# Gate and feature tiles of a decoder layer: wide products by the high weights, narrow ones by the low weights

## The chip, the core and the metric

The kernel runs on one core of a Trainium2 chip. The metric is the device time of one execution in microseconds (us); the time of a kernel is the median of its runs. The engines are TensorE (PE, with its weight loads PEld), VectorE (DVE), ScalarE (ACT), GpSimd (POOL) and SyncE (SP, which issues most of the DMAs). [...]

## What is computed

One layer of a decoder: one projection of the 256 tokens feeds three token mixers (A sparse attention over top-k keys, B dilated windows, C block-sparse, which at 256 tokens is plain causal attention), and a gate per channel merges them. Then come an output projection, a layer norm, a feed-forward part and a second norm.

```
proj = x @ w_in[i]                                    # 256 x 1024 by 1024 x 3528
aq, ak, av, iq, ik, iw, bq, bk, bv, cq, ck, cv = jnp.split(proj, SPLIT_POINTS, axis=-1)
o_a, o_b, o_c = dsa_mixer(...), dilated_mixer(...), moba_mixer(...)
gates = jax.nn.sigmoid(x @ w_gate[i]).reshape(bsz, s_len, N_BRANCH, D_MODEL)
merged = (gates[:, :, 0] * (o_a @ w_br_a[i]) + gates[:, :, 1] * (o_b @ w_br_b[i])
          + gates[:, :, 2] * (o_c @ w_br_c[i]))
x = layer_norm(ALPHA * x + merged @ w_out[i], ln1_g[i], ln1_b[i])
h = jnp.square(jax.nn.relu(x @ w_up[i])) @ w_down[i]
ple = jax.nn.sigmoid(x @ w_ple_gate[i]) * (p[i] @ w_ple[i])
x = layer_norm(ALPHA * x + h + ple, ln2_g[i], ln2_b[i])
```

## The kernel before

All products are float32, made of three products of a shorter type (F32R): every operand is split into a high part and a low part, and high x high, high x low and low x high are summed (function prod, L133 to L135). The low x low product is left out.

The weights come in units of 128 x 1024 (a unit is 128 output channels for all eight k-tiles of 128 inputs). Class Weights moves a unit through: SP loads it (tile raw, L71), ScalarE rounds it to the high part (whi, L75), VectorE and POOL subtract to the low part (wlo, L79; VectorE takes 640 of 1024 columns, POOL the rest). It runs four units ahead of its use; raw and part (whi and wlo) have five buffers each.

x stands transposed in SBUF, tokens along the columns: xh and xl, [128, 8, 256] each. A tile of 128 gate channels (24 of them, fill with "g") or of 128 feature channels (queries and keys, feat) is gemm: for each of the eight k, three products of 256 columns into one half of a PSUM bank of pool mm, which has three banks. ScalarE takes a gate tile out of PSUM through a tanh (L238). A feature tile is split from PSUM into a high half by ScalarE and a low half by VectorE (q_pair L214 and L215, k_pair L225 and L226).

In the up projection (L681 to L686) the tiles are built in another way: x1 holds high and low halves side by side, the high weights multiply both at once in a product of 512 columns, the low weights multiply the high half in one of 256, and VectorE adds the two halves of the bank.

Around the tiles lies attention. logits makes the logits of two heads (L271) into banks b0 to b2. VectorE adds the bias table T and takes the maxima (L357 for mixer B, in slots, L341 for C and A, in head); ScalarE takes the exponentials (L366, L344) and scales them (L333); in mixer B POOL adds up three groups in between (L368 and L369). TensorE transposes the result (L310 to L312), multiplies by the values (L317 to L320), and VectorE adds the halves (L323). Tables T are loaded by SP from DRAM (L182). VectorE also finds the 64 largest entries of the index of mixer A (topk, eight rounds of MAX and MATCH_REPLACE, then am, L440 to L444); POOL adds am to T for the heads of A (ta, L497 and L498).

The order of the instructions on each engine is not the program's: a scheduler of the framework lays out all engines by a model of their times and its priorities, and fixes one order per engine, in which the engines then run, waiting for one another by semaphores. TASKS sets the order of the weight units.

Of the kernel before, what the change touches and what calls it, by code (L numbers as in the profile page):

```python
# [11 lines left out]
F32 = mybir.dt.float32  # L12
F32R = mybir.dt.float32r
ALU = mybir.AluOpType
AF = mybir.ActivationFunctionType
AX = mybir.AxisListType
# [4 lines left out]
S = 256  # L21
KT = D // 128
# [71 lines left out]
def hybrid_layer(ctx: ExitStack, tc: tile.TileContext, x0, xn, pT, wqk, wva, wvb, wg, wbc, wba,  # L94
                 wout, wup, wdq, wdn, wpg, wple, lnrow, rel, onehot, pick, out):
    nc = tc.nc
    pe, act, dve, pool = nc.tensor, nc.scalar, nc.vector, nc.gpsimd
# [8 lines left out]
    W = Weights(tc, raw, part)  # L106
# [24 lines left out]
    def prod(ps, a, b, first, last):  # L131

        pe.matmul(ps, lhsT=a[0], rhs=b[0], start=first, stop=False)  # L133
        pe.matmul(ps, lhsT=a[0], rhs=b[1], start=False, stop=False)  # L134
        pe.matmul(ps, lhsT=a[1], rhs=b[0], start=False, stop=last)  # L135

    def gemm(ps, units, xs, k=0):

        for u in units:
            hi, lo = W.get(u)  # L140
            for o in range(0, hi.shape[1], 128):
                prod(ps, (hi[:, o:o + 128], lo[:, o:o + 128]), xs[k], k == 0, k == len(xs) - 1)
                k += 1
# [5 lines left out]
    right = lambda n, b: one.enter_context(tc.tile_pool(name=n, bufs=b, side="right"))  # L149
    p1, k1, kp = (right(n, b) for n, b in (("p1", 1), ("k1", 2), ("kp", 3)))  # L150

    xh = p1.tile([128, KT, S], F32R, name="xh")
    xl = p1.tile([128, KT, S], F32R, name="xl")
    xs = [(xh[:, k], xl[:, k]) for k in range(KT)]
    n_u = [0]

# [5 lines left out]
    G = pm.tile([128, 24, S], F32, name="G")  # L162
    pm.tile([128, 8], F32, name="apart")
    u_q = [[] for _ in range(FIRST)]

    u_g, u_bc, u_ba, u_out = [], [], [], []
# [38 lines left out]
    def mmbank(shape):  # L205
        t = mm.tile([128, 512], F32, name="mm", tag="mm")
        return t[:, 0:256] if shape == 256 else t
# [11 lines left out]
    def k_pair(a, b=None):  # L219


        k = (kp if b is None else k1).tile([128, 2, S], F32R, name="k", tag="k")
        for d, ps in ((slice(0, 128), a),) if b is None else ((slice(0, 64), a),
                                                             (slice(64, 128), b)):
            act.copy(k[d, 0], ps)  # L225
            dve.tensor_tensor(k[d, 1], ps, k[d, 0].bitcast(F32), op=ALU.subtract)  # L226
        return k

    n_g, n_c = [0], [0]

    def fill(what):


        for w in what:
            if w == "g":
                ps = mmbank(256)
                gemm(ps, u_g[n_g[0]], xs)
                act.activation(G[:, n_g[0]], ps, AF.Tanh, scale=0.5)  # L238
                n_g[0] += 1
                continue  # L240
            f = n_c[0]
            n_c[0] += 1
            hi, lo = W.get(u_bc[f][0])
            ps = mmbank(512).rearrange("p (i s) -> p i s", i=2)
            for i, (k0, k1) in enumerate(((3, 5), (5, 8))):
                for k in range(k0, k1):
                    c = slice((k - 3) * 128, (k - 2) * 128)
                    prod(ps[:, i], (hi[:, c], lo[:, c]), (op[:, k, 0], op[:, k, 1]), k == k0,
                         k == k1 - 1)
            g = G[:, 3 * f + 1:3 * f + 3]  # L250
            dve.scalar_tensor_tensor(g, g, 1.0, ps, op0=ALU.add, op1=ALU.mult)  # L251
            dve.tensor_tensor(g[:, 0], g[:, 0], g[:, 1], op=ALU.add)

    def feat(f):
        ps = mmbank(256)
        gemm(ps, u_q[f], xs)
        if f > 4:
            next(side, None)
        return ps

    def logits(q, k):


        ss = [next(ps_s)[:, 0:384] for _ in range(2)]
        with tc.high_priority(offset=500):
            for b in range(2):
                c = slice(b * 128, (b + 1) * 128)
                for i, (x, y) in enumerate(((1, 0), (0, 0), (0, 1))):
                    for h in (1, 0):
                        d = slice(64 * h, 64 * h + 64)  # L270
                        m = pe.matmul(ss[h][:, QC[b]], lhsT=q[d, x, c],  # L271
                                      rhs=k[d, y, 0:128 * (b + 1)], start=i == 0, stop=i == 2)
                        if b or i or not h:
                            tc.keep_in_program_order(m)
        return ss
# [3 lines left out]
    op = pm.tile([128, 8, 2, S], F32R, name="op")  # L279
# [108 lines left out]
    with ExitStack() as begin:  # L388
# [4 lines left out]
        with tc.high_priority(offset=1000):  # L393
# [4 lines left out]
            for k in range(KT):  # L398
                act.copy(xh[:, k], g0[:, k, 0:S])
                for a, b in cut[k]:  # L400
                    a = max(a, S)
# [4 lines left out]
        for k in range(KT):  # L406
            for i, (w, x) in enumerate(((sh, xh), (sh, xl), (sl, xh))):
                for f in range(FIRST):
                    pe.matmul(first[f], lhsT=w[:, k, 128 * f:128 * f + 128], rhs=x[:, k],  # L409
                              start=k == i == 0, stop=k == KT - 1 and i == 2)  # L410
        iq = [q_pair(ps, 0.125) for ps in first]
    tp, wk, wk2, sm = (right(n, b) for n, b in (("tp", 3), ("wk", 3), ("wk2", 2), ("sm", 6)))
    tab = bias_table()
    ps = feat(4)
    kI, kA = k_pair(ps[0:64], ps[0:64]), k_pair(ps[64:128], ps[64:128])

# [8 lines left out]
    for j in range(4):  # L425
        s = logits(iq[j], kI)
# [9 lines left out]
    def topk():  # L436
        for r in range(TOPK // 8):
            for b in range(2):
                m8 = sm.tile([128, 8], F32, name="m8", tag="m8")
                dve.max(m8, idx[:, QC[b]])  # L440
                dve.match_replace(idx[:, QC[b]], in_to_replace=m8, in_values=idx[:, QC[b]],
                                  imm_value=GONE)
            yield
        dve.tensor_scalar(am, idx, -2e38, -NEG, op0=ALU.is_gt, op1=ALU.mult)  # L444

    side = topk()
# [4 lines left out]
    for j in range(2):  # L451
        ps = feat(5 + 4 * j)
        k = k_pair(ps)
        fill("g")
        qs = []
        for g in range(3):
            qs.append(q_pair(feat(6 + 4 * j + g)))
            if g:
                fill("g")
        o = opair()  # L460
        Ts = [toeplitz(6 + 2 * j + h, 4) for h in range(2)]
        slots(qs, k, Ts, 1 + 2 * j, o)
        pair_out(o, 3 + j)
        fill("g")
# [6 lines left out]
    for j in range(3):  # L471
        ps = feat(13 + 2 * j)
        k = k_pair(ps)
        q = q_pair(feat(14 + 2 * j))
        s = logits(q, k)
# [12 lines left out]
    for j in range(3):  # L488
        q = q_pair(feat(19 + j))
        s = logits(q, kA)  # L490
# [152 lines left out]
    for b in range(2):  # L643
        t = slice(b * 128, (b + 1) * 128)
        for c in range(2):
            cs = slice(c * 512, (c + 1) * 512)
            ps = mmbank(512)
# [28 lines left out]
    for f in range(32):  # L676
        ps = mmbank(512).rearrange("p (b a t) -> p b a t", b=2, a=2)
        hi, lo = W.get(u_up[f][0])
        cs = [slice(k * 128, (k + 1) * 128) for k in range(KT)]
        for k in range(KT):  # L680
            pe.matmul(ps, lhsT=hi[:, cs[k]], rhs=x1[:, :, k], start=k == 0, stop=False)  # L681
        for k in range(KT):
            pe.matmul(ps[:, :, 0], lhsT=lo[:, cs[k]], rhs=x1[:, :, k, 0], start=False,  # L683
                      stop=k == KT - 1)
# [11 lines left out]
        g = four[:, u % 2]  # L696
        act.activation(g[:, :, m], r, AF.Square)
        if m % 2 == 0:
            continue
        hi, lo, y = ((hQ[:, u, 0, 0], hQ[:, u, 0, 1], g[:, 0, 0:2]) if m == 1 else  # L700
                     (hQ[:, u, 1:3, 0], hQ[:, u, 1:3, 1], g[:, :, 2:4]))
# [87 lines left out]
    for i in range(early):  # L789
        x = order[i]  # L790
        hi, lo = W.get(u_dn[i])
# [7 lines left out]
    p1, p5, p6, p7 = (acc["P" + n] for n in "1567")  # L799
# [25 lines left out]
    for b in range(2):  # L825
        for c in range(len(CUT[b])):
            cs = slice(*CUT[b][c])
# [110 lines left out]
```

## Time and profile before

| | |
|---|---|
| time of the runs, median (lowest to highest of 3) | 446.04 us (444.22 to 446.31) |
| time of the profiled execution | 445.0 us |
| its span, from the first to the last instruction | 443.2 us |
| mean granted TensorE clock | 0.994 |
| busy: TensorE, its weight loads | 97%, 88% of the span |
| busy: VectorE, ScalarE, POOL | 75%, 61%, 23% of the span |
| moved by DMA | 84.28 MB, 190 GB/s |

A line of the profile names the source line, the engine, the operation, the output and input tiles (buffer numbers left out), the shape and the count; then come the busy time in us, the mean of one in ns, and the idle time ahead of it with what ended it. The timeline and the chain of waits give start and length in us. TensorE's matmuls are pipelined: one starts while the last is still draining, so their lengths overlap.

### The profile page before, as it was taken

The numbers are of one execution on the slowest core, as the hardware profiler recorded it, in microseconds if no ns is written. First come the engines' busy times: TensorE is split into PE (matmuls) and PEld (weight loads), VectorE is DVE, ScalarE is ACT, GpSimd is POOL, SyncE is SP. The second block draws the span as 40 slices with busy tenths as digits, with TensorE's granted clock in tenths as the row PEclk, the third lists the DMA queues.
The fourth block names the chain that finished last, engine by engine and source line by source line (L and its number), as shares of the span: only waits on it lengthen the run. The fifth ranks groups of instructions, "written<-read, shape, count | busy, mean of one in ns | idle before, by whom it ended". The sixth has DMA issues, their size and how long they took to land.

```text
span 443.2 us, 7744 instructions
## 1 busy us (share of the span) xinstructions
PE 429.7 (97%) x2839; PEld 389.3 (88%) x2839; DVE 333.7 (75%) x601; ACT 270.7 (61%) x488; POOL 102.8 (23%) x99
## 2 busy tenths in 40 slices
PE   8999999998999999999999999999999999999992
PEld 8989999998999989999886888888888888888882
DVE  5867977536546568759958769999888978689956
ACT  6765366476877758756604657878877765455500
POOL 2764247378533545500001000000000000000001
PEclk9999999999999999999999999999999999999997
DMA  8895956448635326468870766567655364656502
GB/s 302 298 314 156 286 160 199 150 113 281 224 94 170 126 77 184 131 202 315 260 283 0 248 226 193 190 191 270 204 189 184 100 207 132 228 195 212 215 0 95
DMA packets 27146, 84.28 MB, mean 190 GB/s; under 512 B 2864, under 2 KB 6872, under 8 KB 26724
## 3 DMA queue, kind: packets, MB, share of 16 engines
q1 hardware_dynamic: 25872, 79.54, 54.4%
q10 hardware_dynamic: 1140, 4.19, 2.6%
q8 instruction: 22, 0.36, 0.3%
q14 instruction: 16, 0.13, 0.1%
q0 software_dynamic: 96, 0.06, 0.0%
HBM read 81.88 MB, written 1.90 MB: 189 GB/s over the span
## 4 chain that ended last, share of the span: by engine, by line
PE 89%; DVE 3%; issue 2%; DMA 2%; POOL 2%; ACT 1%; SPq 0%; POOLq 0%; DVEq 0%
PE mm L681 13%; PE mm L133 12%; PE mm L135 12%; PE mm L134 12%; PE b L133 8%; PE b L135 8%; PE b L134 8%; PE mm L683 7%; PE b L271 3%; PE b L409 3%; DMA T<-tabd 1%; DMA pr<-in_pT_dram 1%; PE b L129 1%; DVE st L605 1%; DVE Y L622 1%
## 5 line engine op out<-in xcount | busy, mean ns | idle before, releaser
L75 ACT CAST whi<-raw 128x1024 fp32r<-128x1024 f32 (+3 forms) x147 | 148.0, 1013 | 81.2 <-issue 19.9
L79 DVE TENSOR_TENSOR wlo<-raw,whi 128x1024 fp32r<-128x1024 f32 (+5 forms) x147 | 156.1, 1076 | 42.7 <-ACT whi L75 38.7
L79 POOL TENSOR_TENSOR wlo<-raw,whi 128x384 fp32r<-128x384 f32 (+3 forms) x58 | 78.5, 1359 | 83.2 <-ACT whi L75 74.0
L133 PE MATMUL mm<-xh,whi 128*128 128x256 f32 x336 | 95.0, 283 | 1.0 <-DVE G L251 1.0
L135 PE MATMUL mm<-xh,wlo 128*128 128x256 f32 x336 | 95.6, 285 | 0.0
L134 PE MATMUL mm<-xl,whi 128*128 128x256 f32 x336 | 94.7, 282 | 0.0
L133 PEld LDWEIGHTS mm<-xh,whi 128*128 128x128 f32 x336 | 63.3, 189 | 1.5 <-DVE G L251 1.2
L681 PE MATMUL mm<-x,whi 128*128 128x512 f32 x256 | 64.1, 392 | 0.0
L135 PEld LDWEIGHTS mm<-xh,wlo 128*128 128x128 f32 x336 | 63.3, 188 | 0.8
L134 PEld LDWEIGHTS mm<-xl,whi 128*128 128x128 f32 x336 | 63.3, 188 | 0.3
L612 POOL TENSOR_TENSOR rs<-rs,half 128x1 f32<-128x1 f32 x4 | 4.1, 1028 | 244.5 <-DVE rs L611 244.5
L681 PEld LDWEIGHTS mm<-x,whi 128*128 128x128 f32 x256 | 46.1, 189 | 8.3
L683 PEld LDWEIGHTS mm<-x,wlo 128*128 128x128 f32 x256 | 34.9, 190 | 2.5
L683 PE MATMUL mm<-x,wlo 128*128 128x256 f32 x256 | 35.7, 282 | 0.0
L134 PE MATMUL b<-wlo,hT 128*128 128x512 f32 (+1 forms) x88 | 33.4, 380 | 0.0
L135 PE MATMUL b<-whi,hT 128*128 128x512 f32 (+1 forms) x88 | 33.4, 379 | 0.0
L133 PE MATMUL b<-whi,hT 128*128 128x512 f32 (+1 forms) x88 | 31.9, 379 | 0.0
L686 DVE TENSOR_REDUCE r<-mm 128x256 f32<-128x512 f32 x32 | 22.0, 687 | 6.0 <-PE mm L683 6.0
L742 DVE TENSOR_TENSOR raw<-raw 128x1024 f32<-128x1024 f32 x12 | 14.7, 1222 | 9.0 <-DMA raw<-in_wdq_dram 9.0
L133 PEld LDWEIGHTS b<-whi,hT 128*128 128x128 f32 x88 | 16.6, 188 | 3.1
L135 PEld LDWEIGHTS b<-whi,hT 128*128 128x128 f32 x88 | 16.5, 188 | 3.2
L134 PEld LDWEIGHTS b<-wlo,hT 128*128 128x128 f32 x88 | 16.5, 188 | 3.1
(194 smaller groups left out, 782.0 us busy)
## 6 DMA issues: line engine op xcount, KB each, us to landing
raw<-in_wup_dram SPq DMA_DIRECT2D x32, 512.0 KB
raw<-in_wg_dram SPq DMA_DIRECT2D x24, 512.0 KB
raw<-in_wdn_dram SPq DMA_DIRECT2D x20, 512.0 KB
raw<-in_wqk_dram SPq DMA_DIRECT2D x18, 512.0 KB
raw<-in_wdq_dram SPq DMA_DIRECT2D x12, 512.0 KB
raw<-in_wout_dram SPq DMA_DIRECT2D x8, 512.0 KB
raw<-in_wpg_dram SPq DMA_DIRECT2D x8, 512.0 KB
T<-tabd SPq DMA_DIRECT2D x24, 128.0 KB
```

The lines of the kernel that those rows point to most:

```text
L75: nc.scalar.copy(hi, r)
L79: e.tensor_tensor(lo[:, c], r[:, c], hi[:, c].bitcast(F32), op=ALU.subtract)
L129: pe.transpose(t[:, 0:128], ident, ident)
L133: pe.matmul(ps, lhsT=a[0], rhs=b[0], start=first, stop=False)
L134: pe.matmul(ps, lhsT=a[0], rhs=b[1], start=False, stop=False)
L135: pe.matmul(ps, lhsT=a[1], rhs=b[0], start=False, stop=last)
L271: m = pe.matmul(ss[h][:, QC[b]], lhsT=q[d, x, c], rhs=k[d, y, 0:128 * (b + 1)], start=i == 0, stop=i == 2)
L409: pe.matmul(first[f], lhsT=w[:, k, 128 * f:128 * f + 128], rhs=x[:, k], start=k == i == 0, stop=k == KT - 1 and i == 2)
L681: pe.matmul(ps, lhsT=hi[:, cs[k]], rhs=x1[:, :, k], start=k == 0, stop=False)
L683: pe.matmul(ps[:, :, 0], lhsT=lo[:, cs[k]], rhs=x1[:, :, k, 0], start=False, stop=k == KT - 1)
L686: dve.tensor_reduce(r, ps.rearrange("p b a t -> p b t a"), axis=AX.X, op=ALU.add)
L742: dve.tensor_tensor(t[n], t[x], t[y], op=ALU.subtract)
```

## The change

x2 takes the place of xh and xl: one tile [128, 8, 2, 256] with the high and the low half of x side by side for each k, of which xh and xl are views. Two unnamed tiles of 72 and 56 columns stand before and after it. A new function both makes a tile as the up projection does: eight products of 512 columns with the high weights, then eight of 256 with the low weights onto the first half of the bank. Gate tiles and features 5 to 21 use it. VectorE adds the halves of the bank (tensor_reduce over the last axis): for a gate into G, where ScalarE then takes the tanh from SBUF; for a feature into a new tile qs of two buffers, from which q_pair and k_pair then read. Feature 4 stays as it was.

```
-    xh = p1.tile([128, KT, S], F32R, name="xh")
-    xl = p1.tile([128, KT, S], F32R, name="xl")
+    p1.tile([128, 72], F32, name="shift")
+    x2 = p1.tile([128, KT, 2, S], F32R, name="x2")
+    p1.tile([128, 56], F32, name="shift2")
+    xh, xl = x2[:, :, 0], x2[:, :, 1]
...
+    def both(units):
+        ps = mmbank(512)
+        hi, lo = W.get(units[0])
+        cs = [slice(k * 128, (k + 1) * 128) for k in range(KT)]
+        for k in range(KT):
+            pe.matmul(ps, lhsT=hi[:, cs[k]], rhs=x2[:, k].rearrange("p a s -> p (a s)"),
+                      start=k == 0, stop=False)
+        for k in range(KT):
+            pe.matmul(ps[:, 0:S], lhsT=lo[:, cs[k]], rhs=xh[:, k], start=False,
+                      stop=k == KT - 1)
+        return ps.rearrange("p (a s) -> p s a", a=2)
...
             if w == "g":
-                ps = mmbank(256)
-                gemm(ps, u_g[n_g[0]], xs)
-                act.activation(G[:, n_g[0]], ps, AF.Tanh, scale=0.5)
+                ps = both(u_g[n_g[0]])
+                g = G[:, n_g[0]]
+                dve.tensor_reduce(g, ps, axis=AX.X, op=ALU.add)
+                act.activation(g, g, AF.Tanh, scale=0.5)
...
     def feat(f):
-        ps = mmbank(256)
-        gemm(ps, u_q[f], xs)
-        if f > 4:
-            next(side, None)
-        return ps
+        if f == 4:
+            ps = mmbank(256)
+            gemm(ps, u_q[f], xs)
+            return ps
+        ps = both(u_q[f])
+        next(side, None)
+        s = wk2.tile([128, S], F32, name="qs", tag="qs")
+        dve.tensor_reduce(s, ps, axis=AX.X, op=ALU.add)
+        return s
```

The scheduler lays out every engine anew. Lines behind feat are 20 higher in the changed kernel (L310 becomes L330). On TensorE, the first transposes of mixer B (of the exponentials eb of the first slot pair) stand before among gate products:

```order
L133 MATMUL mm<-xh,whi 128x256
L134 MATMUL mm<-xl,whi 128x256
L135 MATMUL mm<-xh,wlo 128x256
L310 MATMUL b_898<-ident,eb 128x128
L311 MATMUL b_898<-ident,eb 128x128
L312 MATMUL b_898<-ident,eb 128x128
```

At the same place now (x_113 is x2, L237 the wide and L240 the narrow product):

```order
L330 MATMUL b_854<-ident,eb 128x128
L331 MATMUL b_854<-ident,eb 128x128
L332 MATMUL b_854<-ident,eb 128x128
L240 MATMUL mm<-x_113,wlo 128x256 x3
L237 MATMUL mm<-x_113,whi 128x512 x8
L240 MATMUL mm<-x_113,wlo 128x256 x8
L237 MATMUL mm<-x_113,whi 128x512 x4
L337 MATMUL b_860<-pth_117,V 128x256
```

Ahead of these transposes there stood 11 tiles behind feature 4 and seven groups of logits; now 13.6 tiles and eight groups do. On VectorE, the end of topk for mixer A, before:

```order
L79 TENSOR_TENSOR wlo<-raw,whi 128x640
L441 MATCH_REPLACE idx<-m_1119,idx 128x128
L441 MATCH_REPLACE idx<-m_1122,idx 128x256
L440 MAX m_1193<-idx 128x8
L440 MAX m_1196<-idx 128x8
L441 MATCH_REPLACE idx<-m_1193,idx 128x128
L441 MATCH_REPLACE idx<-m_1196,idx 128x256
```

And now (L253 and L278 are the two new reductions, L384 the maxima of the first slot pair that its exponentials wait for, L364 before):

```order
L253 TENSOR_REDUCE G<-mm 128x256
L384 TENSOR_REDUCE mx<-mxb 128x2 x2
L79 TENSOR_TENSOR wlo<-raw,whi 128x640
L460 MAX m_1044<-idx 128x8
L461 MATCH_REPLACE idx<-m_1041,idx 128x128
L461 MATCH_REPLACE idx<-m_1044,idx 128x256
L278 TENSOR_REDUCE qs<-mm 128x256
L460 MAX m_1102<-idx 128x8
L460 MAX m_1105<-idx 128x8
L351 RECIPROCAL r<-den 128x2
L461 MATCH_REPLACE idx<-m_1102,idx 128x128
```

The reductions stand between the rounds of topk, and the maxima L384, which stood behind its last round, now stand ahead of its last two; ten reductions are ahead of them in the queue. On POOL, the second slot pair of mixer B (eb_1244 and eb_1245 are its two heads, T_2174 the table of the first three heads of A), before:

```order
L368 TENSOR_TENSOR eb_1244<-eb_1244 128x384
L497 TENSOR_TENSOR ta_2178<-T_2174,am_125 128x128
L498 TENSOR_TENSOR ta_2178<-T_2174,am_125 128x256
L497 TENSOR_TENSOR ta_2264<-T_2174,am_125 128x128
L498 TENSOR_TENSOR ta_2264<-T_2174,am_125 128x256
L369 TENSOR_TENSOR eb_1244<-eb_1244 128x384
L368 TENSOR_TENSOR eb_1245<-eb_1245 128x384
```

And now:

```order
L388 TENSOR_TENSOR eb_1148<-eb_1148 128x384
L517 TENSOR_TENSOR ta_1984<-T_1980,am_126 128x128
L518 TENSOR_TENSOR ta_1984<-T_1980,am_126 128x256
L389 TENSOR_TENSOR eb_1148<-eb_1148 128x384
L388 TENSOR_TENSOR eb_1149<-eb_1149 128x384
L517 TENSOR_TENSOR ta_2063<-T_1980,am_126 128x128
L518 TENSOR_TENSOR ta_2063<-T_1980,am_126 128x256
L79 TENSOR_TENSOR wlo_1331<-raw_1328,whi_1330 128x384
```

One pair of ta instead of two stands ahead of the first head's second sum (L369, now L389). On SP the last six loads of tables T and the load of pr (the input p) now stand behind two more weight loads than before.

## The prediction

> **What bounds the kernel now.** I read the page first: the engines' shares, then the chain that ended last.
>
> ```profile
> span 443.2 us, 7744 instructions
> ...
> PE 429.7 (97%) x2839; PEld 389.3 (88%) x2839; DVE 333.7 (75%) x601; ACT 270.7 (61%) x488; POOL 102.8 (23%) x99
> ...
> PE 89%; DVE 3%; issue 2%; DMA 2%; POOL 2%; ACT 1%; SPq 0%; POOLq 0%; DVEq 0%
> ```
>
> TensorE is busy in 97% of the span, and the chain is 89% TensorE. So time comes off where TensorE issues less, or where it waits less, and nowhere else. The gate and feature tiles lie in its first half, up to 200 us. I cut that stretch into windows:
>
> ```profile
> core 0: us, PE busy (x) PEld busy (x) DVE busy (x) ACT busy (x) POOL busy (x), PEclk, DMA share, GB/s
> 33.00:63.00 30.00, 30.00 (x271) 28.55 (x268) 26.90 (x101) 14.48 (x25) 10.43 (x8) 1.00 0.66 200
> 63.00:85.00 22.00, 22.00 (x198) 21.27 (x197) 12.83 (x34) 13.43 (x29) 13.61 (x11) 1.00 0.55 182
> 85.00:110.00 25.00, 22.89 (x170) 22.35 (x167) 13.05 (x27) 16.02 (x30) 18.44 (x18) 1.00 0.63 186
> 110.00:160.00 50.00, 50.00 (x439) 48.94 (x439) 27.07 (x78) 36.09 (x93) 22.71 (x18) 1.00 0.46 149
> 160.00:205.00 45.00, 43.98 (x380) 43.24 (x379) 34.20 (x71) 29.84 (x65) 16.53 (x14) 1.00 0.56 172
> ```
>
> The columns to compare are the window's length, PE and DVE. PE is idle for 25.00 - 22.89 = 2.1 us around the second slot pair and 45.00 - 43.98 = 1.0 us in the last window: 3.1 us in 172. The granted clock is 1.00 throughout. VectorE is full in only one window, 33 to 63 us (26.90 of 30); over all five it is busy 114.05 of 172 us.
>
> A busy matmul says little here, since its 280 ns overlap the next one. The spacing of starts is what counts, so I took that from the timeline, the second row being the 46th matmul after the first, all of 256 columns:
>
> ```profile
> 127.97 0.28 PE L134 MATMUL mm<-xl,whi 128*128 128x256 f32 x1
> ...
> 133.40 0.28 PE L134 MATMUL mm<-xl,whi 128*128 128x256 f32 x1
> ```
>
> (133.40 - 127.97) / 46 = 0.1180 us each. For 512 columns the chain of waits has runs of equal matmuls, with start and length:
>
> ```profile
> 246.41 0.91 PE b L133 x4
> ...
> 268.29 1.84 PE mm L681 x8
> 270.13 0.95 PE mm L683 x8
> ```
>
> Four 512-column products with contiguous columns take 0.91 us, 0.2275 each. The two rows below are a tile of the up projection, which is already built as the change builds its tiles: 8 wide and 8 narrow products in 1.84 + 0.95 = 2.79 us. Its columns are read in two pieces of 128, not contiguously.
>
> **The change part by part.**
>
> *The products.* 24 gates and 17 features (5 to 21; feature 4 stays) are 41 tiles. Before, a tile is 24 x 0.1180 = 2.832 us. After, the wide operand is x2[:, k], 512 contiguous columns, so I take the row of the contiguous products: 8 x 0.2275 + 8 x 0.1180 = 2.764 us. That saves 0.068 us a tile, 2.8 us in all. The number of columns is the same (768 per k); what goes is one start in three. The lower bound is the up tile as it stands, 2.79: 0.042 x 41 = 1.7 us. The upper end is the 2.8 itself, as no row shows a shorter spacing.
>
> [...]
>
> *The sums on VectorE.* Each tile adds one reduction of 128x512 to 128x256. The up stage has the same one, and its activation from SBUF; beside it the gate's from PSUM and the two halves of a query:
>
> ```profile
> L686 DVE TENSOR_REDUCE r<-mm 128x256 f32<-128x512 f32 x32 | 22.0, 687 | 6.0 <-PE mm L683 6.0
> ...
> L687 ACT ACTIVATE r<-r 128x256 f32<-128x256 f32 x32 | 13.3, 416 | 9.2 <-DVE r L686 9.2
> ...
> L238 ACT ACTIVATE G<-mm 128x256 f32<-128x256 f32 x24 | 9.1, 379 | 0.1
> ...
> L215 DVE SCALAR_TENSOR_TENSOR q<-mm,q 128x256 fp32r<-128x256 f32 x12 | 5.0, 413 | 0.0
> ...
> L214 ACT ACTIVATE q<-mm 128x256 fp32r<-128x256 f32 x12 | 4.6, 380 | 0.0
> ```
>
> VectorE's neighbours overlap by some 0.08 us, as these rows show (0.35 long, yet the next starts 0.27 later):
>
> ```profile
> 61.12 0.35 DVE L444 TENSOR_SCALAR am<-idx 128x384 f32<-128x384 f32 x1
> 61.39 0.22 DVE L364 TENSOR_REDUCE mx<-mxb 128x2 f32<-128x6 f32 x2
> ```
>
> So a reduction is 0.61 us of VectorE's queue, 41 x 0.61 = 25 us, and its load in the five windows goes from 114 to 139 of 172 us. ScalarE pays 24 x 0.037 = 0.9 us for the gates from SBUF, and as little for the queries and keys. Both lie beside TensorE as long as VectorE keeps up. What is late if it doesn't: a PSUM bank of mm is now freed by the reduction and not by ScalarE, and TensorE waits for it three tiles on, so two tiles (5.5 us) are the cover. A query also comes one reduction later, but in the new order at least one whole other tile (2.8 us) stands between a query tile and its logits, against 0.61 + 0.38 + 0.41 us for reduction and halves. I cost all of this at nothing.
>
> The tight place is the first pair's softmax, at the end of VectorE's full window. There the maxima are ready at L364 (61.39 above), and TensorE transposes the result at 67.4:
>
> ```profile
> L310 PE MATMUL b<-ident,eb x4: 270/286/302, 67.4 to 106.3; 128*128 128x128 f32 x4
> ```
>
> That chain takes 6.0 us. In the new order ten reductions stand ahead of the maxima (6.1 us, of which VectorE's idle 3.1 us in that window can absorb half), so they come 3.0 to 6.1 us later. TensorE in turn reaches the transposes 2.6 tiles and one group of logits later (13.6 tiles after feature 4 stand ahead, where 11 did): 2.6 x 2.76 + 0.9 = 8.1 us. The cover is 2 to 5 us.
>
> *The moved order.* The waits of TensorE in the table of waits (total, times, longest) and the chain ahead of them:
>
> ```profile
> PE b L310 <- POOL wlo L79: 1.4, 1, 1.4
> PE mm L133 <- DVE G L251: 1.0, 1, 1.0
> PE b L310 <- issue: 0.8, 1, 0.8
> PE b L133 <- ACT x L634: 0.5, 2, 0.2
> PE b L135 <- DVE x L635: 0.4, 1, 0.4
> ```
>
> ```profile
> 87.83 4.84 DMA T<-tabd
> 92.67 0.07 issue
> 92.73 0.47 POOL ta L497
> ...
> 94.44 1.04 POOL ta L497
> ...
> 96.13 1.02 POOL eb L369
> ...
> 97.17 0.80 ACT eb L333 x2
> ...
> 100.92 3.35 DMA pr<-in_pT_dram
> ```
>
> At 97 us the transposes wait for POOL's sum eb, which stands behind two pairs of ta, which wait for a table T. The second pair costs 96.13 - 94.44 = 1.7 us. In the new order one pair stands there, so the wait of 0.8 to 0.9 us goes. At 105 us the other head's transposes wait 1.4 us, behind ScalarE's copy of pr and POOL's queue:
>
> ```profile
> 104.86 0.62 ACT L467 CAST ph<-pr 128x512 fp32r<-128x512 f32 x1 [3.58 <-DMA pr<-in_pT_dram]
> ```
>
> That copy now comes after both heads' scalings, but SP loads the last tables T behind two more weight loads, and POOL's ta wait for them. I leave this wait as it is, and the 1.0 us behind L251 too. Bounds for all waits in the windows: all gone, -3.1 us; as much again, +3.1. The first layer norm's order changes too; its waits are 0.5 + 0.4 us, taken as unchanged, bounds -0.9 and +0.9. The two shift tiles and qs move addresses and nothing that a row prices: 0, bounded by the 0.9 of that norm either way.
>
> *Sum.* -2.8 - 0.9 = -3.7 us: 445.0 - 3.7 = 441.3 for the profiled execution (span 443.2 and 1.8 around it). It lies 1.0 below the median 446.04 of the runs, so the median becomes 442.3.
>
> **The rivals.**
>
> *Slower: VectorE becomes the bound from 33 to 85 us.* For it: 26.90 of 30 busy there before anything is added. Against: the load over the five windows stays at 139 of 172, and the cover above. It decides where the reductions cost so much that the maxima come over 8.1 us late: ten of them at over 0.81 + 0.31 = 1.1 us each, against the 0.61 seen. To lose more than 0.5% it must cost 6 us on TensorE (at 1.7 us each): 446.04 - 2.8 + 6 = 449.2.
>
> *A wide product saves less.* The spacing is that of the up stage, 1.7 us, and no wait goes: 446.04 - 1.7 = 444.3. For it: those are the only tiles of this shape in the trace. Against: their columns come in pieces. [...]
>
> *The waits move instead of going.* Tables T and pr, now behind weight loads on SP, keep ta, and so eb and the transposes, 2.5 us longer (one table took 4.84 to land): 446.04 - 2.8 + 2.5 = 445.7. For it: SP's new order. Against: TensorE also comes there 3 us later.
>
> **How the numbers follow.** A change of 0.5%, 2.2 us, is about what a measurement of this kernel tells from no change: below 443.8 is faster, above 448.3 slower. My forecast has 0.6, the slow VectorE 0.1, the lesser saving 0.2 and the moved waits 0.1. So faster 0.6, same 0.3, slower 0.1. The predicted time is 442.3. The low end takes all waits away (446.04 - 2.8 - 3.1 = 440.1, rounded to 440); the high end holds the moved waits and the unknown of the norm (445.7 + 0.9 = 446.6); 449.2 is left out.
>
> **What would show it.** After: runs of eight wide products at 1.82 us (1.84 would be the rival's) and of eight narrow ones at 0.94; 24 and 17 reductions near 690 ns on VectorE; VectorE above 25 busy microseconds more; TensorE's waits in the table below 4 us and none longer than 1 us for a reduction. A wait of TensorE for a reduction or for a late transposed softmax near 75 us would show the slow rival, and a longer idle around 95 to 110 us the moved waits. Wrong altogether would be a reduction from the mm banks that takes over 1 us, or a spacing of 0.236 us for the wide products.

## Result: 1.2% slower, and the profile after

The changed kernel takes 450.25 us (median of 6 runs, 449.12 to 451.90), beside 445.46 for the kernel before (6 runs). The ratio is 1.012, with a 95% interval of 1.0101 to 1.0139. I had forecast 442.3 and no more than 446.6.

The profiled execution of the changed kernel took 449.12 us, that of before 445.0, so 4.1 of the 4.8 us can be looked for in the traces. First the page: span, engines, and the chain that ended last.

```profile
span 447.3 us, 7129 instructions
...
PE 428.9 (96%) x2511; PEld 372.7 (83%) x2511; DVE 367.0 (82%) x642; ACT 274.7 (61%) x488; POOL 92.9 (21%) x99
...
PE 85%; DMA 6%; issue 2%; DVE 2%; POOL 2%; ACT 1%; SPq 0%; POOLq 0%; DVEq 0%; ACTq 0%
```

328 matmuls fewer, TensorE's busy time hardly less, and the chain has passed from 89% TensorE to 85%, with 6% DMA where there were 2%. The stretches of the prediction, and the one behind them that I had not cut (its row of before stands last):

```profile
core 0: us, PE busy (x) PEld busy (x) DVE busy (x) ACT busy (x) POOL busy (x), PEclk, DMA share, GB/s
33.00:63.00 30.00, 30.00 (x204) 24.91 (x201) 28.19 (x83) 14.11 (x23) 9.58 (x9) 1.00 0.70 211
63.00:85.00 22.00, 22.00 (x146) 19.34 (x145) 21.13 (x67) 14.12 (x28) 11.10 (x11) 1.00 0.65 193
...
110.00:160.00 50.00, 47.34 (x307) 41.52 (x308) 37.64 (x89) 37.05 (x92) 16.84 (x17) 0.97 0.47 155
...
205.00:240.00 35.00, 31.18 (x161) 26.39 (x162) 29.17 (x44) 14.55 (x21) 1.01 (x1) 1.00 0.74 249
```

```profile
205.00:240.00 35.00, 34.40 (x176) 28.83 (x175) 29.62 (x47) 16.07 (x24) 2.01 (x2) 1.00 0.65 229
```

TensorE stays full from 33 to 85 us, where VectorE has become full (28.19 of 30 and 21.13 of 22). It is idle for 2.7 us from 110 to 160 us, where it had no idle time, and for 3.8 us from 205 to 240 us, where it had 0.6. In the windows between, its idle time fell: from 2.1 to 1.5 us (85 to 110) and from 1.0 to 0.1 us (160 to 205). The table of waits names the places (total, times, longest):

```profile
PE b L337 <- DVE o L343: 2.7, 1, 2.7
PE b L135 <- DVE q L593: 2.1, 1, 2.1
...
PE mm L133 <- ACT op L346: 1.1, 1, 1.1
PE b L291 <- DVE q L217: 0.8, 1, 0.8
PE b L401 <- DMA relt<-in_pick_dram: 0.8, 1, 0.8
PE b L133 <- ACT q L592: 0.7, 1, 0.7
PE b L337 <- ACT pth L333: 0.7, 1, 0.7
```

No row waits for a reduction (L253, L278); TensorE's weight loads wait for them 0.7 us in all, never over 0.2 us at a time.

To split the whole difference I took the starts of all matmuls from the trace. The spacing to the next start, less the undisturbed one of that width (0.118 us for 256 columns, 0.227 for 512, 0.108 for 128, 0.173 for 384, 0.151 for 328), is an excess. Over 0.3 us I count it as a wait, from 0.025 to 0.3 as slow matmuls, and the rest belongs to the products. Some records are missing, so a column is good to about 0.5 us.

| kernel | median (before beside it), us | ratio, 95% | span | products | waits | slow |
|---|---|---|---|---|---|---|
| before | | | 443.2 | 416.2 | 4.9 | 12.3 |
| changed | 450.25 (445.46) | 1.0101 to 1.0139 | 447.3 | 414.4 | 10.0 | 13.1 |
| layout_only | 446.77 (444.66) | 1.0028 to 1.0055 | 443.4 | 417.3 | 5.1 | 11.2 |
| layout_no_shift | 445.07 (444.92) | 0.9993 to 1.0016 | 443.4 | 416.2 | 6.5 | 10.9 |
| early_pr | 453.61 (444.66) | 1.0162 to 1.0211 | 453.0 | 414.6 | 13.6 | 15.0 |
| old_last_gates | 449.48 (444.66) | 1.0098 to 1.0137 | 447.2 | 414.9 | 6.5 | 16.1 |
| early_pr_old_last | 451.36 (444.66) | 1.0133 to 1.0170 | 449.2 | 414.7 | 10.1 | 14.6 |
| pr_mid | 446.22 (445.16) | 1.0010 to 1.0046 | 443.1 | 414.5 | 6.1 | 12.7 |
| pr_mid_old_last | 446.53 (445.16) | 1.0007 to 1.0037 | 442.8 | 414.9 | 4.3 | 13.8 |
| gates_only | 449.32 (445.16) | 1.0067 to 1.0112 | 447.2 | 415.7 | 9.0 | 12.1 |
| features_only | 446.70 (445.16) | 1.0014 to 1.0044 | 445.3 | 416.3 | 6.5 | 12.7 |
| pr_mid_no_sums | 444.58 (444.92) | 0.9980 to 1.0006 | 441.8 | 414.8 | 2.4 | 14.2 |
| pr_mid_old_last_late_xn | 442.79 (444.92) | 0.9938 to 0.9973 | 440.8 | 414.9 | 3.1 | 13.0 |
| mended_no_shift | 442.85 (445.20) | 0.9920 to 0.9960 | 440.7 | 415.5 | 3.7 | 11.7 |
| changed_no_shift | 450.44 (445.20) | 1.0093 to 1.0143 | 446.7 | 415.2 | 8.3 | 13.3 |
| before_late_xn | 446.17 (445.20) | 1.0003 to 1.0031 | 444.8 | 416.3 | 6.6 | 12.1 |

For the changed kernel: products 1.8 us less, waits 5.1 more, slow matmuls 0.8 more, together 4.1, the difference of the spans. By place, all waits over 0.3 us of the kernel before are gone (0.9, 1.5 and 1.2 us at 97, 105 and 161 us, 1.3 us at 238 to 243 us), and 10.0 us of others have come: 4.6 us at 105 to 115 us, 4.4 us at 204 to 218 us, and 1.0 us at 25 us for a load of the bias table (relt, L401). That last one is not of the new order: it is 0.6 us in layout_only, which has the old order, and under 0.3 us in pr_mid and changed_no_shift, which have the new one at this place.

### The two places

**The second slot pair, 105 to 117 us.** ScalarE's timeline there (start, length, and in brackets the idle time ahead with its releaser):

```profile
107.64 0.42 ACT L216 ACTIVATE q<-qs 128x256 fp32r<-128x256 f32 x1 [0.27 <-DVE qs L278]
111.00 0.62 ACT L487 CAST ph<-pr 128x512 fp32r<-128x512 f32 x1 [2.94 <-DMA pr<-in_pT_dram]
111.53 1.04 ACT L75 CAST whi<-raw 128x1024 fp32r<-128x1024 f32 x1
112.60 0.37 ACT L342 COPY ov<-b 64x256 f32<-64x256 f32 x1
...
113.42 0.48 ACT L333 CAST pth<-b 128x384 fp32r<-128x384 f32 x1
```

The copy of p waits for its load, and behind it in ScalarE's queue stand ov, which empties the first head's result out of PSUM, and pth of the second head. The chain of waits (start, length) shows both ends:

```profile
105.78 5.20 DMA pr<-in_pT_dram
...
112.95 1.02 DVE wlo L79
...
114.31 0.41 DVE o L343
...
114.86 0.55 PE b L337
```

SP issues the load of p at 105.78, behind two more weight loads and two more loads of T than before, and it takes 5.20 us to land (3.35 before). For one of these loads of T, at 103.31, SP had stood until POOL was done with an older table:

```profile
SPq L184 <- POOL ta L518: 1.4, 1, 1.4
```

The load's buffer is not what held it. In this kernel p shares its two buffers with the exponentials eb; the first head's were read last by its transposes at 101.1 us, and the second head's are still to be read, at 107.8 us, when p is issued. VectorE's o (L343) follows ov and a weight's low half. TensorE's first product by the values of the second head needs the PSUM bank that o empties, and it starts 2.8 us late. Behind the wait the granted clock falls to about half, and slow matmuls cost 3.6 us from 110 to 160 us, against 2.1 before:

```profile
112.00:114.00 2.00, 0.20 (x2) 0.00 (x0) 2.00 (x3) 1.83 (x4) 0.99 (x1) 1.00 1.03 416
114.00:116.00 2.00, 1.14 (x5) 1.17 (x6) 2.00 (x10) 0.58 (x3) 0.00 (x0) 0.61 0.73 225
116.00:118.00 2.00, 2.00 (x8) 1.71 (x7) 1.78 (x5) 2.00 (x6) 1.08 (x1) 0.53 0.60 229
118.00:120.00 2.00, 2.00 (x14) 1.78 (x14) 0.58 (x2) 1.98 (x8) 0.57 (x1) 1.00 0.23 33
```

**The end of the stage, 201 to 218 us.** In TensorE's new order 66 branch products stand behind the last head's products by the values; before, 102 did. The last head is also finished later (VectorE's low half op, after, then before), and TensorE has less to do until then:

```profile
205.99 0.42 DVE L347 TENSOR_TENSOR op<-o,op 128x256 fp32r<-128x256 f32 x1 [0.47 <-ACT op L346]
```

```profile
199.76 0.42 DVE L327 TENSOR_TENSOR op<-o,op 128x256 fp32r<-128x256 f32 x1
```

TensorE waits for op (1.1 us) and then, with the loads of wout late as well, for the first halves of the merged tiles. The chain:

```profile
204.76 4.33 DMA raw<-in_wout_dram
...
209.11 1.06 ACT hT L75
...
214.36 0.67 DVE wlo L79
...
217.15 0.43 DVE q L593
...
217.62 1.19 PE b L135 x4
```

### The profile page after: what moved, and what is told of

It reads as the page before. It is cut to its first block, busy times and chain, and to the rows that moved or that the text cites. A ratio compares the mean times of both kernels' runs of the same rounds, so it can differ in the third digit from the quotient of the medians.

```text
span 447.3 us, 7129 instructions
## 1 busy us (share of the span) xinstructions
PE 428.9 (96%) x2511; PEld 372.7 (83%) x2511; DVE 367.0 (82%) x642; ACT 274.7 (61%) x488; POOL 92.9 (21%) x99
## 4 chain that ended last, share of the span: by engine, by line
PE 85%; DMA 6%; issue 2%; DVE 2%; POOL 2%; ACT 1%; SPq 0%; POOLq 0%; DVEq 0%; ACTq 0%
PE mm L237 16%; PE mm L701 13%; PE mm L240 8%; PE b L135 8%; PE b L133 8%; PE b L134 8%; PE mm L703 7%; PE mm L133 4%; PE mm L134 4%; PE mm L135 3%; PE b L291 3%; DMA raw<-in_wva_dram 2%; DMA G<-in_x_dram 1%; DMA relt<-in_pick_dram 1%; DMA pr<-in_pT_dram 1%
## 5 line engine op out<-in xcount | busy, mean ns | idle before, releaser
L79 DVE TENSOR_TENSOR wlo<-raw,whi 128x1024 fp32r<-128x1024 f32 (+5 forms) x147 | 163.0, 1121 | 16.1 <-ACT whi L75 14.7
L237 PE MATMUL mm<-x,whi 128*128 128x512 f32 x328 | 87.1, 399 | 0.0
L79 POOL TENSOR_TENSOR wlo<-raw,whi 128x384 fp32r<-128x384 f32 (+3 forms) x58 | 66.7, 1160 | 94.1 <-ACT whi L75 67.7
L237 PEld LDWEIGHTS mm<-x,whi 128*128 128x128 f32 x328 | 58.2, 190 | 10.4 <-DVE qs L278 0.2
L701 PE MATMUL mm<-x,whi 128*128 128x512 f32 x256 | 64.1, 392 | 0.0
L701 PEld LDWEIGHTS mm<-x,whi 128*128 128x128 f32 x256 | 46.1, 189 | 8.3
L240 PE MATMUL mm<-x,wlo 128*128 128x256 f32 x328 | 48.2, 284 | 0.0
L240 PEld LDWEIGHTS mm<-x,wlo 128*128 128x128 f32 x328 | 45.4, 191 | 3.4
L703 PEld LDWEIGHTS mm<-x,wlo 128*128 128x128 f32 x256 | 34.9, 190 | 2.5
L703 PE MATMUL mm<-x,wlo 128*128 128x256 f32 x256 | 35.7, 282 | 0.0
L133 PE MATMUL mm<-op,whi 128*128 128x256 f32 x64 | 18.0, 286 | 1.1 <-ACT op L346 1.1
L707 ACT ACTIVATE r<-r 128x256 f32<-128x256 f32 x32 | 13.3, 416 | 9.2 <-DVE r L706 9.1
```

Of the source, the lines that this page charges most:

```text
L79: e.tensor_tensor(lo[:, c], r[:, c], hi[:, c].bitcast(F32), op=ALU.subtract)
L237: pe.matmul(ps, lhsT=hi[:, cs[k]], rhs=x2[:, k].rearrange("p a s -> p (a s)"), start=k == 0, stop=False)
L240: pe.matmul(ps[:, 0:S], lhsT=lo[:, cs[k]], rhs=xh[:, k], start=False, stop=k == KT - 1)
```

## The experiments

My first theory after the result: the loss is in these two places, where the new order waits. The rivals: VectorE's added load itself (it would show as another wait wherever one is taken away), and the addresses, moved by x2 and the two shift tiles.

### layout_only, layout_no_shift, changed_no_shift: x2 and the addresses

layout_only is before with this edit; layout_no_shift leaves out the two shift lines; changed_no_shift is the changed kernel without them.

```
-    xh = p1.tile([128, KT, S], F32R, name="xh")
-    xl = p1.tile([128, KT, S], F32R, name="xl")
+    p1.tile([128, 72], F32, name="shift")
+    x2 = p1.tile([128, KT, 2, S], F32R, name="x2")
+    p1.tile([128, 56], F32, name="shift2")
+    xh, xl = x2[:, :, 0], x2[:, :, 1]
```

> The kernel before with x2 and the two shift tiles in place of xh and xl, all products and sums as before; the order on every engine but for one step of TensorE is that of before. If the new order and its waits make the loss (my theory), this has none of it: 445.5 us, within 0.7 of before, TensorE's gaps as before (6.3 us over 120 ns each). If the addresses cost the time (rival), it is near the changed kernel, 449 to 450, with VectorE's operations longer at the same order.

> layout_only without the two shift tiles of 72 and 56 columns: the order on every engine is that of layout_only, only addresses differ. layout_only was 1.8 us (0.4%) over before, with a profile as long as that of before. If the shift's addresses do that: within 0.5 us of before, 444.5 to 445.7. If it is x2 itself, high and low half side by side, or something else: 446 to 447.2 as layout_only.

> The changed kernel without the two shift tiles, the order on every engine unchanged. Shift theory (it costs 1.7 us wherever it stands): 450.25 - 1.7 = 448.5 us (447.8 to 449.3). Otherwise 450.25 as the changed kernel: then all its loss is the order's.

Measured: 446.77, 445.07 and 450.44 us. layout_only is 2.1 us over its own kernel before, three times what I had allowed. In the old order the two shift tiles cost 1.7 us; in the changed order they cost nothing (450.25 with them, 450.44 without). The addresses therefore are not the cause of the changed kernel's loss. Where they cost time in the old order the waits don't tell: the profiles of layout_only and layout_no_shift have the same span, 443.4 us, and I took a second one of layout_only.

> layout_only once more, for a second profile. Its runs lie at 445.2 to 446.0 and at 446.6 to 447.7, and the first profile was of the low group (445.17). If this execution is of the high group, and the cause is the load of the down projection's weights that features_only shows (TensorE waits 1.6 us near 397 us), the wait table holds such a row and the span is 1.5 to 2 us longer; otherwise the excess lies elsewhere. If it is of the low group again, nothing follows.

That execution took 446.03 us, with a span of 444.2. Its waits are those of before (behind the start the longest is 1.5 us, at 105 us), and none lies near 397 us. The products hold the better lead: 417.3 us in both profiles of layout_only, 416.2 in layout_no_shift and before. From 33 to 205 us the median spacing of the products with x is 120 ns in layout_only, both times, and 117 in layout_no_shift. In the changed order the shift tiles make the narrow products slower (120 against 117 ns) but the wide ones faster (231 ns in the changed kernel, 233 in changed_no_shift), and there the products take 0.8 us less with them. So the addresses move the spacing by 2 or 3 ns, one way or the other by the width. Why, and what makes the rest of the 1.7 us, stays open.

### early_pr, old_last_gates, early_pr_old_last: the first attempt at the two places

early_pr loads p early into a tile of its own (the remarks in the code are mine, here and below):

```
-            nc.sync.dma_start(t[:, i], bass.AP(
+            last[1] = nc.sync.dma_start(t[:, i], bass.AP(      # each load of a table T
...
-    pr = wk2.tile([128, 2, S], F32, name="pr", tag="eb")
-    nc.sync.dma_start(pr, pT)
...
+        if j == 0:
+            pr = p1.tile([128, 2, S], F32, name="pr")
+            with tc.issue_after(last[1]):
+                nc.sync.dma_start(pr, pT)
         slots(qs, k, Ts, 1 + 2 * j, o)
```

old_last_gates makes the last three gates as before (LASTG is 21):

```
+                if n_g[0] >= LASTG:
+                    ps = mmbank(256)
+                    gemm(ps, u_g[n_g[0]], xs)
+                    act.activation(G[:, n_g[0]], ps, AF.Tanh, scale=0.5)
+                    n_g[0] += 1
+                    continue
```

> The changed kernel with p (tile pr) loaded into a tile of its own behind the first slot pair's tables, so that ScalarE's copy ph no longer stands at 111 us between the two heads of the second slot pair; the rest of ScalarE's queue is that of the changed kernel. Theory (the loss is two places where the new order waits): the waits of L337 at 105 and 112 us (0.8 + 2.8 us) and the half-speed matmuls behind them (0.8) go, 450.25 - 4 = 446.3 us (445.8 to 447.5), TensorE's busy share in the window 110 to 160 us back to over 49 of 50. Rival (VectorE's added 28 us are the bound): TensorE finds the next late sum instead, 449.5 to 450.5.

> The changed kernel with the last three gates (21 to 23) made as before, 24 products of 256 columns and no reduction. In the order the last head's products by the values then have 99 branch products behind them, as before (102), and not 66. Theory: the waits at 204 to 217 us (1.25 + 0.85 + 2.28 us for op and q) fall to under 1 us, the three tiles give back 0.13 us: 450.25 - 3.5 = 446.8 us (446 to 448). Rival (VectorE's load): three reductions of 41 are 2 us of VectorE's time, so at most 0.4 us is gained: 449.8.

> Both edits together: p loaded early, and the last three gates as before. Theory: both places are gone and the rest of the wide products' 1.7 us shows: 450.25 - 4 - 3.5 = 442.8 us (442 to 444.5), 1 to 3 us under before. Rival (VectorE's load): 449 or more, with the waits elsewhere.

Measured: 453.61, 449.48 and 451.36 us. By its numbers the theory missed all three, while the rival (VectorE's load) had 449.8 for the second and 449 or more for the third. The traces tell what happened. In early_pr the wait at the second slot pair fell from 2.8 to 0.8 us, but the scheduler had moved the copy ph forward with the load. The load was issued at 42.49 and took 7.53 us, ScalarE stood 9.8 us for it, and TensorE 5.1 us for the indexer's ri behind the copy (waits, then the chain):

```profile
PE b L291 <- ACT ri L450: 5.1, 1, 5.1
```

```profile
42.49 7.53 DMA pr<-in_pT_dram
...
50.04 0.63 ACT ph L489
```

In old_last_gates the waits from 204 to 218 us fell from 4.4 to 2.0 us, but the 2.0 us were followed by half-clock matmuls, 3.2 us of slow ones from 205 to 262 us against 0.6 in the changed kernel:

```profile
213.00:215.00 2.00, 2.00 (x6) 1.56 (x6) 2.00 (x6) 2.00 (x3) 0.00 (x0) 0.52 0.81 258
215.00:217.00 2.00, 2.00 (x7) 1.52 (x7) 2.00 (x3) 1.66 (x4) 0.00 (x0) 0.63 0.60 242
```

So each run has another long wait or half-clock matmuls in place of what it took away, which is also what the rival had said. From these three runs alone the two can't be told apart; the next one does it.

### pr_mid: the load early, the copy where p has landed

```
-    act.copy(ph, pr)
+    with tc.issue_after(last[0]):          # the second slot pair's last query
+        act.copy(ph, pr)
```

> The changed kernel with p loaded into a tile of its own behind the first slot pair's tables, as in early_pr, but with ScalarE's copy ph queued behind the last query of the second slot pair, some 35 us later than in early_pr, where p has long landed. TensorE's and POOL's orders are those of the changed kernel, on ScalarE and VectorE only ph and pl move. In early_pr the copy itself waited (5.3 us of TensorE at 49 us), but TensorE's wait at the second slot pair fell from 2.8 to 0.8 us. Theory (places where the order waits): here both are gone, and the half-clock matmuls behind the long wait too: 450.25 - 2 - 1.4 = 446.9 us (446 to 448), clock 1.00 from 110 to 160 us. Rival (VectorE's load is the bound): another wait for VectorE of the same size takes its place, 449.5 or more.

The load of p is moved as in early_pr. Measured: 446.22 us, as the theory expected. TensorE's and POOL's orders are those of the changed kernel, on SP only the load of p has moved, on ScalarE and VectorE only ph and pl, and 3.7 of the 4.8 us are gone (4.8 over before in the first comparison, 1.1 in this one). All 41 sums are still there, and the rival's 449.5 or more did not come. From 110 to 160 us:

```profile
110.00:160.00 50.00, 49.79 (x331) 43.69 (x332) 39.32 (x93) 38.27 (x96) 18.81 (x18) 1.00 0.47 154
```

49.79 of 50 busy against 47.34, clock 1.00 against 0.97. Its waits:

```profile
PE b L135 <- DVE q L596: 2.1, 1, 2.1
...
PE mm L133 <- ACT op L346: 1.1, 1, 1.1
PE b L291 <- DVE q L217: 0.8, 1, 0.8
PE b L337 <- ACT pth L333: 0.8, 1, 0.8
```

The end of the stage is as it was, now at 201 to 213 us. The place of one load in SP's queue, with the copy behind it in ScalarE's, is shown to be the largest part of the loss. How much is the load's and how much the copy's is not split, as the edit moves both. Between the two profiles the waits fell by 3.9 us: 2.8 us are the wait at 112 us, 1.0 us is that for relt at 25 us, which is none of this edit's.

### gates_only and features_only: one half of the change each

gates_only has feat as in the kernel before, features_only has the gates' part of fill as before.

> Only the gates are made in the new way, the features as before; x2 and the shift tiles stay. In its order 66 branch products stand behind the last head's products by the values, as in the changed kernel (before 102), and p's copy ph stands ahead of both heads' halves of the second slot pair. Theory (places): the waits at 204 to 217 us come as in the changed kernel, 4 to 5 us, and the one at 112 us; 24 tiles save 1.0 us: 448.5 to 450.5 us. Rival (VectorE's load, 24 of 41 reductions): 24/41 of the changed kernel's loss, 444.7 + 0.6 * 5.5 = 448 us, spread over the stage.

> Only the features 5 to 21 are made in the new way, the gates as before; x2 and the shift tiles stay. In its order 89 branch products stand behind the last head's products by the values, and p's copy ph stands behind the first head's transposed half, as before. Theory (places): little of both waits, 17 tiles save 0.7 us: 444.5 to 447 us. Rival (VectorE's load): 17 reductions of 0.61 us, most of them in the window where VectorE is full (33 to 85 us), so as much as the gates cost or more, 447 to 449 us, with TensorE waiting near 67 or 75 us.

Measured: 449.32 and 446.70 us, both inside what the places gave. In gates_only this is in part luck: of the 2.8 us expected near 112 us only 1.0 came (at 109), and 1.5 us at 100 and 1.7 us at 159 us were not foreseen. gates_only has the end of the stage of the changed kernel (waits of 1.25, 0.8 and 2.3 us from 203 to 216 us), with 24 reductions; features_only, with 17, loses little over a third as much (1.5 against 4.2 us), and its longest wait, 1.8 us at 397 us, lies far behind the features. By the load alone it would be 17/24, 2.9 us.

### pr_mid_no_sums: what VectorE's sums cost

```
-                g = G[:, n_g[0]]
-                dve.tensor_reduce(g, ps, axis=AX.X, op=ALU.add)
-                act.activation(g, g, AF.Tanh, scale=0.5)
+                act.activation(G[:, n_g[0]], ps[:, :, 0], AF.Tanh, scale=0.5)
...
-        s = wk2.tile([128, S], F32, name="qs", tag="qs")
-        dve.tensor_reduce(s, ps, axis=AX.X, op=ALU.add)
-        return s
+        return ps[:, :, 0]
```

> pr_mid without the 41 reductions: the gates' tanh and the halves of queries and keys read the first half of the bank only, so the product of the high weights with the low half of x is computed and left out of the result. All products stay. In its order 91 branch products stand behind the last head's products by the values (pr_mid 66, before 102). If VectorE's sums, through the order they lead to, make what is left of the loss (theory): the waits at 201 to 211 us (1.2 + 0.6 + 2.3 us) fall to 1 to 1.5 us and the one for a query at 109 us (1.0) goes: 446.2 - 3.5 = 442.7 us (441.7 to 444). If the sums cost nothing as I predicted: 446.2, within 0.7.

Measured: 444.58 us, 1.6 under pr_mid (1.4 if each is compared with its own kernel before). Waits fell as expected, from 6.1 to 2.4 us:

```profile
PE b L133 <- ACT q L591: 0.8, 1, 0.8
PE b L287 <- DVE q L217: 0.8, 1, 0.8
PE b L133 <- ACT x L653: 0.3, 1, 0.3
```

But slow matmuls rose by 1.5 us, at 63 to 85 and 205 to 262 us, and the theory's 3.5 is missed by half. So 41 sums, with the order that they lead to and the queries read from SBUF, cost some 1.5 us, not 0 and not 3.5. Even without them this kernel only equals before.

### pr_mid_old_last, pr_mid_old_last_late_xn, mended_no_shift, before_late_xn: the end of the stage

The first is pr_mid with the edit of old_last_gates. In the second the load of xn waits for its turn behind the merged tiles' halves, and the third leaves out the shift tiles too. before_late_xn is the kernel before with this edit alone (the row load of the norm, which moves along, is issued at 219 us or later in both kernels):

```
-    act.dma_start(PL, xn)
-    row_load(rows1, 0)
+    with tc.issue_after(last[0]):          # the halves of the second merge
+        act.dma_start(PL, xn)
+        row_load(rows1, 0)
```

> pr_mid with the last three gates made as before. In old_last_gates the waits at 204 to 217 us fell from 4.4 to 2.0 us, but 2.5 us of slowed matmuls came behind them. Theory: 444.7 (before) - 1.7 for the wide products + 1 (TensorE's wait for a query at the second slot pair) + 2 to 4 (the wait for the output projection's operand and the matmuls slowed behind it) = 446 to 448 us, that is 0 to 1 us under pr_mid. Rival (VectorE's load): 449 or more.

> pr_mid_old_last with the load of xn (tile PL, 1 MB, on ScalarE's queue) behind the halves of the second merged pair, some 10 us later, out of the way of the loads of wout. In pr_mid_old_last ScalarE waits for wout at 207 us, and TensorE 1.9 us for the query-like operand behind it, with 1 us of slowed matmuls after. If the two loads share the DMA engines there (theory): that wait falls under 0.7 us, 446.5 - 2 = 444.5 us (443.5 to 445.5). If the loads of wout are late for their buffers, freed late by VectorE (rival): 446.5, or slower if the first norm now waits for xn.

> pr_mid_old_last_late_xn without the two shift tiles, the order on every engine unchanged. If the shift's addresses cost 1.7 us on their own (446.77 against 445.07 in layout_only and layout_no_shift): 442.8 - 1.7 = 441.1 us (440.5 to 442), 0.7 to 1.0% under before. If the shift's cost belongs to the old order only: 442.8.

> The kernel before with the load of xn queued late, as in pr_mid_old_last_late_xn. If that load cost only the changed order (theory: before has no wait over 0.5 us between 161 and 237 us), it stands at before, 444.9, within 0.7, or up to 1 us slower where its new order waits for the halves. If the gain of that edit is its own, 443 us.

Measured: 446.53, 442.79, 442.85 and 446.17 us. The old last gates alone do nothing again (446.22 without them). ScalarE's timeline in the first and in the second kernel shows what the first one waits for:

```profile
206.59 1.05 ACT L76 CAST hT<-raw 128x1024 fp32r<-128x1024 f32 x1 [3.87 <-DMA raw<-in_wout_dram]
```

```profile
202.97 1.05 ACT L76 CAST hT<-raw 128x1024 fp32r<-128x1024 f32 x1 [0.27 <-DMA raw<-in_wout_dram]
```

With the 1 MB of xn out of the way the load of wout is there 3.6 us earlier, and TensorE's wait of 1.8 us behind it is gone from the table. SP issues the loads of wout at the same times in both (198.86, 201.26 and 204.32 us in the first, 198.83, 201.24 and 204.30 in the second); the one of 198.86, issued 0.1 us behind xn, takes 7.66 us to land. So it was the other load that kept wout, and not a buffer freed late. Against before, the gain is 3.5 us by the medians (1.4 over, 2.1 under); the spans of the profiles, 442.8 and 440.8, account for 2.0 of it (the first was one of the fastest runs of its kernel). The kernel is 0.45% faster than before (ratio 0.9955, 0.9938 to 0.9973). mended_no_shift is as fast (0.994, 0.992 to 0.996): its expected 1.7 us for the shift tiles did not come. In the kernel before the same edit loses 1.0 us by the medians, and it has waits of 0.8 and 1.3 us at 211 and 217 us that before has not; the gain belongs to the changed order, not to before. The early load of p was not tried in the kernel before, where the wait of 1.5 us at 105 us also stands behind the copy ph. So it is not shown how much of the 2.1 us is the wide products' and how much before could have had from that load.

## Why the prediction was wrong, step by step

The forecast was -3.7 us, the spans say +4.1. Of these 7.8 us the products make 1.0 (-1.8 for -2.8), TensorE's waits 6.0 (+5.1 for -0.9; 1.0 of it is the wait for relt, which is chance), and the slow matmuls 0.8, for which the sum had no term.

**The products: right in kind, at the lower bound.** 2.8 us was forecast with the row of contiguous columns (0.2275), with 1.7 as the bound by the up projection's tile. The chain of the changed kernel has the up projection's numbers:

```profile
97.34 1.84 PE mm L237 x8
99.18 0.95 PE mm L240 x8
```

1.84 + 0.95 = 2.79 us a tile, and 1.8 us in all by the table. The nearest row was that of the same tile, not that of contiguous columns.

**The sums: right in size, wrong at "nothing".** They are as long as the row of the up projection said (687 ns):

```profile
L253 DVE TENSOR_REDUCE G<-mm 128x256 f32<-128x512 f32 x24 | 16.4, 681 | 3.0 <-PE mm L240 2.8
L278 DVE TENSOR_REDUCE qs<-mm 128x256 f32<-128x512 f32 x17 | 11.6, 682 | 4.8 <-PE mm L240 4.8
L217 DVE SCALAR_TENSOR_TENSOR q<-qs,q 128x256 fp32r<-128x256 f32 x12 | 7.2, 600 | 0.0
```

The cover held where I had tested it: the first slot pair's transposes wait nowhere, with VectorE full from 33 to 85 us. The rival with VectorE as the bound there was rightly put low. What was missed: the sums also weigh in the scheduler's order, which leaves the last head 66 products of cover instead of 102, where I had looked at no row. And a query read from SBUF costs 600 ns in the mean instead of 413. At 108.7 us one takes 1.22 us, and TensorE waits 0.8 us for it. Three of the twelve take 1019 to 1234 ns (at 72.0, 74.5 and 108.7 us), and these are the three that start while POOL is at work on a wlo (L79, from 71.32, 74.03 and 108.08 us on); the others take 399 to 426. In the kernel before, where one input is mm in PSUM, all twelve (L215) take 400 to 418, though nine of them start while POOL is at work on a wlo. The traces show when it is long, not why.

**The moved order: the step that failed.** I took 0.9 us off for the pair of ta, and that wait went as forecast; the others of before went too, which I had not forecast. Of the wait at 105 us I wrote "I leave this wait as it is", though the cause was in front of me: on SP the last tables and p stand behind two more weight loads, as the section on the change says, and the sentence ahead of it carries this to POOL's ta only. What I did not follow is ScalarE's queue behind the copy. I saw that ph stands behind both heads' scalings and took that for harmless. It stands ahead of ov and pth, so the whole second head hangs on the load. The bounds for the waits (-3.1 to +3.1) were the waits of before, and a new wait in a place that had none is not bounded by them: waits grew by 5.1 us and dragged half-clock matmuls behind them. The wait of 2.8 us at 112 us and the slow matmuls behind it went when p's load and copy were moved (pr_mid, 3.7 us).

**The rival that was right.** "The waits move instead of going" named the place (a longer idle around 95 to 110 us; it came at 105 to 115), the loads and the queue. It was given 2.5 us and 0.1. The way was another, through ph, ov and pth and not through ta and eb. Moving load and copy gained 3.7 us, and the end of the stage was not in it.

**The windows.** I cut the trace up to 205 us because the changed tiles end there. The wait that the shorter cover caused came at 201 to 218 us.

## What to carry to other kernels

Before costing a change at its own lines, follow in the new order each load that has moved: what is queued on the engine that consumes it, and who needs the rows behind that. A bound from the waits of the old kernel holds only for an order that stays. And when the products are already at 97% of the span, a saving of 1.8 us can be lost to a single load that is issued later in its queue; look for such loads first, since mending two of them (p and xn), with the last three gates made as before, made this kernel 0.5% faster than before instead of 1.2% slower. How much of that 0.5% is this change's own is not shown.

## What the runs showed of the hardware

Waits of much the same length did not have the same price. After 2.8 us of waiting at 112 us, and after 2.0 us at 210 us in old_last_gates, the granted clock was at half for some 3.4 us (rows of 2 us at 0.61 and 0.53, and at 0.52 and 0.63, are half speed for 1.6 + 1.9 and 1.9 + 1.5 us). After 2.3 us at 211 us in pr_mid it stayed at 1.00:

```profile
211.00:213.00 2.00, 0.28 (x2) 0.00 (x0) 2.00 (x4) 1.03 (x1) 0.00 (x0) 1.00 0.68 225
213.00:215.00 2.00, 1.59 (x7) 1.33 (x8) 2.00 (x5) 1.77 (x5) 0.00 (x0) 1.00 0.89 313
```

In the changed kernel's record of the granted clock the half speed behind the wait at 112 us lasts 3.413 us, with 109.226 us at full speed ahead of it and 324.266 us behind it. A wait of the same 2.3 us at 219 us in early_pr was followed by half speed (mean clock 0.95 from 205 to 240 us, against 1.00 in pr_mid). So the length of a wait does not tell alone whether half speed follows; what else it takes is not shown.
